# The even layer's output projection begun with the attention's half of its contraction, and the convolution's layer norm written behind that half

## The chip, the cores and the metric

The kernel runs on one core of a Trainium2 chip. The time is device microseconds (us) of that core for one execution. The engines are called PE (TensorE, the matmuls), PEld (its weight loads, which overlap the matmuls), DVE (VectorE), ACT (ScalarE), POOL (GpSimd) and SP (SyncE, which here only issues transfers).

## The reference: what is computed

Two residual layers on 512 positions of width 1024 and a final norm. The change lies in the first, the even layer. Its two halves are gated, concatenated and mapped back by one matrix:

```python
o_b = mla(...) * jax.nn.silu(z_b)
o_a = conformer_conv(glu_a, glu_g, conv_w, conv_b, ln_g, ln_b) * jax.nn.silu(z_a)
return x + (jnp.concatenate([o_b, o_a], axis=-1) @ w_out)

def conformer_conv(a, g, w, bias, ln_g, ln_b):
    u = a * jax.nn.sigmoid(g)
    u = dw_conv(u, w) + bias
    return jax.nn.silu(layer_norm(u, ln_g, ln_b))
```

`o_b` (the attention) and `o_a` (the convolution) are 512 x 1024 each, and `w_out` is 2048 x 1024: rows 0 to 1023 of it meet `o_b`, rows 1024 to 2047 meet `o_a`. All numbers are float32.

## The kernel before, in words

Each float32 operand of a projection is split into a rounded part and a rest (`hi`, `lo`), and a product is three matmuls: hi by hi, lo by hi, hi by lo. Weights come in slabs of 128 x 1024 (512 KB). `Weights._prepare` does for each slab: a transfer into `w_raw` on SP's queue (L84), a cast to `w_hi` on ACT (L87), and the rest `w_lo` on DVE or POOL (L88; in this projection by turns, odd and even places in the list of slabs). There are 2 buffers of `w_raw` and 3 each of `w_hi` and `w_lo`; `Weights.next` prepares one slab ahead of the one it hands out. So a slab's transfer waits until the `w_lo` of the slab two before is made, and its cast waits until PE has read the `w_hi` of the slab three before.

The output projection of the even layer is `mm_tm("oe", ...)`. It is done for the two halves h = 0, 1 of the 1024 output columns, with 8 slabs each; a slab holds two of the 16 blocks of 128 rows of the contraction. For each slab there are 4 tiles of 128 positions with 6 matmuls each (4 that read `w_hi`, 2 that read `w_lo`), 24 a slab. Slabs 0 to 3 of half h = 0 meet the attention's blocks (their split parts are the tiles `o_s`), slabs 4 to 7 the convolution's (`o_hi`, `o_lo`). Half h = 0 adds up in the banks `acc`, `acc`, `acc`, `cv`, half 1 in `sb`, `sb`, `tp`, `tp`.

Ahead of it stands the layer norm of the convolution's output, for 8 tiles of 128 channels (`ct`), L642 to L649: two DVE operations with one operand in PSUM (L644, L645), two on ACT (L646, L647), one on DVE with two operands in SBUF (L648), and the product with the gate on POOL (L649). Then each of the 8 tiles is split (`split_pages`: a cast on ACT at L358, a difference on DVE or POOL at L359). The gates themselves come from four matmul groups, the last of which (`gate_a(6)`, `gate_a(7)`) stand on PE right ahead of the projection.

The program is written in one order and each engine gets its instructions from a scheduler that may move them, but each engine then runs its list strictly in order, and waits where an instruction's inputs or buffers aren't ready. An instruction's wait holds up all behind it on that engine. SP's list is of the same kind.

Of the kernel before, what the change touches and what calls it, by code (L numbers as in the profile page):

```python
# [10 lines left out]
AF = mybir.ActivationFunctionType  # L11
ALU = mybir.AluOpType
# [91 lines left out]
OUT_E = (list(range(8)), [4, 5, 6, 7, 0, 1, 2, 3])  # L104
# [66 lines left out]
def trunk(ctx, tc, A, out, dbg=None):  # L171
    nc = tc.nc
    V, G, SC, T = nc.vector, nc.gpsimd, nc.scalar, nc.tensor
# [12 lines left out]
    def page(name, tag, dt=F32):  # L186
        return pg.tile([P, S], dt, name=name, tag=tag, bufs=npage[tag])
# [4 lines left out]
    def small(shape, name, bufs=2, dt=F32):  # L192
        return cp.tile(shape, dt, name=name, tag=name, bufs=bufs)
# [7 lines left out]
    def bank(tag):  # L201
        return ps.tile([P, S], F32, name=tag, tag=tag, bufs=banks[tag])

    def four(which):

        tags = [t for t in banks for _ in range(banks[t])]
        return tags[:4] if which == 0 else tags[4:]
# [61 lines left out]
    def along(cols, tag):  # L269

        b = bank(tag)
        for t in range(NT):
            T.matmul(b[:, t * P:(t + 1) * P], cols[:, t:t + 1].broadcast_to([P, P]), ident, start=t == 0, stop=t == NT - 1,
                     skip_group_check=True)
        return b

    def halves_square(part, x, h):

        j = small([P, S], "junk", bufs=1, dt=BF16)
        SC.activation(j, x[:, h * S:(h + 1) * S], AF.Square, accum_out=part[:, h:h + 1])  # L280
        if h == 0:
            mean_eps(part[:, 2:3], part[:, 0:1], D)
        else:
            V.tensor_scalar(part[:, 3:4], part[:, 1:2], 1.0 / D, part[:, 2:3], op0=ALU.mult, op1=ALU.add)
# [10 lines left out]
    def big(name):  # L295
        return bg.tile([P, KT, S], F32R, name=name, tag="big", bufs=2)

    def normT(x_tiles, gain, parts, tags):

        hi, lo = big("xT_hi"), big("xT_lo")  # L300
        for t in range(NT):
            r, tt = rstd(x_tiles[t], parts[t]), slice(t * P, (t + 1) * P)
            for h in range(2):
                c, hh, kk = page("xn", "keep"), slice(h * S, (h + 1) * S), slice(4 * h, 4 * h + 4)
                V.scalar_tensor_tensor(c, x_tiles[t][:, hh], r, gain[h], op0=ALU.mult, op1=ALU.mult)
                tp = transposed([c[:, k * P:(k + 1) * P] for k in range(4)], tags[t % 2][h])
                split_psum(hi[:, kk, tt], lo[:, kk, tt], tp.rearrange("p (k l) -> p k l", k=4))
        return [hi[:, k] for k in range(KT)], [lo[:, k] for k in range(KT)]
# [9 lines left out]
            T.matmul(a, l, r, start=n == 0, stop=n == 3 * kk - 1)  # L318
        return a

    def mm_tm(key, xT, nslabs, n, tags, last=1):


        xh, xl = xT
        accs = [bank(t) for t in tags] if nslabs > last else [None] * NT
        steps, k0 = [], 0
        for s in range(nslabs):
            w = W.next(key)
            steps.append((k0, *w))
            k0 += w[0].shape[1]  # L330
            if nslabs - last <= s < nslabs - 1:
                continue
            for t in range(NT):
                if accs[t] is None:
                    accs[t] = bank(tags[t])
                tt = slice(t * P, (t + 1) * P)
                for i, (k1, wh, wl) in enumerate(steps):
                    kk = range(wh.shape[1])
                    seq = [(x[k1 + k][:, tt], wh[:, k]) for k in kk for x in (xh, xl)]
                    seq += [(xh[k1 + k][:, tt], wl[:, k]) for k in kk]  # L340
                    end = s == nslabs - 1 and i == len(steps) - 1
                    for c, (l, r) in enumerate(seq):
                        T.matmul(accs[t][:, :n], l, r, start=k1 == 0 and c == 0, stop=end and c == len(seq) - 1)  # L343
                if s == nslabs - 1:
                    yield t, accs[t]
            steps = []
# [6 lines left out]
    def split_pages(src, new, pair=None):  # L353

        hs, ls = [], []
        for n, o in enumerate(src):
            hi, lo = (b[:, n] for b in pair) if pair and n < KT else (new(), new())
            SC.copy(hi, o)  # L358
            (V if n % 3 else G).tensor_tensor(lo, o, hi.bitcast(F32), op=ALU.subtract)  # L359
            hs.append(hi)  # L360
            ls.append(lo)
        return hs, ls
# [23 lines left out]
    for t in range(NT):  # L386
        for h in range(2):
            j = small([P, S], "junk", bufs=1, dt=BF16)
# [6 lines left out]
    for b in range(2):  # L395
        for t, a in mm_tm("qkv", xg, 3, 336, four(b)):
            SC.activation(qkv[t][:, b * 336:(b + 1) * 336], a[:, :336], AF.Copy, scale=r4[:, t:t + 1])

    rb = along(r4, "cv")
    xT = [], []  # L400
# [22 lines left out]
    for nm, o, w in (("q_norm", 0, 384), ("kv_norm", 384, 256)):  # L423
        ss = small([P, 4], "ss")
        rs = small([P, 4], "rs")
        for t in range(NT):
            j = small([P, S], "junk", bufs=1, dt=BF16)
# [20 lines left out]
    lg = cp.tile([P, 4, 8], F32, name="lg")  # L448
# [4 lines left out]
    def glu():  # L453

        pa, pgt = mm_cm("a", xT), mm_cm("g", xT)
        ut = page("u", "keep")
        SC.activation(ut, pgt, AF.Tanh, scale=0.5)
        V.scalar_tensor_tensor(ut, ut, 1.0, pa, op0=ALU.add, op1=ALU.mult)
        return ut
# [36 lines left out]
    def up_proj():  # L496

        q_tm = pg.tile([P, NT, 2, 192], F32, name="q_tm", tag="m6", bufs=2)
        v_tm = pg.tile([P, NT, 256], F32, name="v_tm", tag="v", bufs=2)
        for t, a in mm_tm("uq", cT["q_norm"], 2, 384, ("acc",) * 4, 2):  # L500
            SC.activation(q_tm[:, t].rearrange("p j d -> p (j d)"), a[:, :384], AF.Copy, scale=QS)
        for j in range(2):
            qr = q_tm[:, :, j, NOPE:2 * NOPE].rearrange("p t (i d) -> p t i d", i=2)
            rope(qr, qr, [P, NT, 2, ROPE], cosb, sinb, "q")
        for t, a in mm_tm("uv", cT["kv_norm"], 1, 256, ("acc",) * 4):
            SC.copy(v_tm[:, t], a[:, :256])
        return q_tm, v_tm
# [50 lines left out]
    def weigh(prs, allp, v_tm, h0):  # L558

        o = bank("acc")  # L560

        def mms(k):
            for j, pt in enumerate(allp[k]):
                T.matmul(o[j * HD:(j + 1) * HD], v_tm[:, k, (h0 + j) * HD:(h0 + j + 1) * HD], pt,  # L564
                         start=k == 0, stop=k == NT - 1, skip_group_check=True)

        for k in range(NT):
            if k + 2 < NT:
                allp.append(turn(prs, k + 2))
            mms(k)  # L570
        return o

    oT = [None] * 16
    u = [glu(), glu()]

    def gate_a(ct):
        z = mm_cm("za", xT)
        oT[8 + ct] = page("oT", "keep")
        gate(oT[8 + ct], z)
# [11 lines left out]
    for p in range(8):  # L591
# [22 lines left out]
        o = weigh(prs, allp, v_tm, h0)  # L614
# [8 lines left out]
    ob = split_pages(oT[:8], lambda: page("o_s", "att", F32R))  # L623
# [15 lines left out]
    lb = [along(rs[:, h], "sb") for h in range(2)]  # L639
    gate_a(6)  # L640
    gate_a(7)
    for ct in range(8):  # L642
        th, v, y = page("ln_th", "att"), page("ln_v", "att"), u[ct]
        V.tensor_tensor(y, y, lb[0], op=ALU.mult)  # L644
        V.tensor_tensor(y, y, lb[1], op=ALU.subtract)  # L645
        SC.activation(th, y, AF.Tanh, bias=lg[:, 1, ct:ct + 1], scale=lg[:, 0, ct:ct + 1])  # L646
        SC.activation(v, y, AF.Identity, bias=lg[:, 3, ct:ct + 1], scale=lg[:, 2, ct:ct + 1])  # L647
        V.scalar_tensor_tensor(v, th, 1.0, v, op0=ALU.add, op1=ALU.mult)  # L648
        G.tensor_tensor(oT[8 + ct], oT[8 + ct], v, op=ALU.mult)  # L649


    oh, ol = (a + b for a, b in zip(ob, split_pages(oT[8:], None, (big("o_hi"), big("o_lo")))))
    x1 = []
    for t in range(NT):
        x1.append(wide("x1"))
# [1 line left out]
    parts = [small([P, 4], "part", bufs=4) for _ in range(NT)]  # L657
    for h in range(2):
        c = slice(h * S, (h + 1) * S)
        o = [[p[2 * i + j] for i in OUT_E[h] for j in range(2)] for p in (oh, ol)]  # L660
        for t, a in mm_tm("oe", o, 8, 512, four(h), 2 if h else 1):
            V.tensor_tensor(x1[t][:, c], a, x1[t][:, c], op=ALU.add)
            halves_square(parts[t], x1[t], h)
    if dbg == "even":
# [13 lines left out]
    xT = normT(x1, gain, parts, (("cv", "acc"), ("acc", "acc")))  # L678
# [118 lines left out]
    for d in range(2):  # L797
        tp = transposed([d1[:, t, d * SH:(d + 1) * SH] for t in range(NT)], "tp", SH)
        cs = tmp("cs", "c5", 3)[:SH]
        for c in range(NT):  # L800
            o, i, z = cs[:, c * P:(c + 1) * P], tp[:, c * P:(c + 1) * P], ident[:SH]
            if d:
                o, i = o[:, ::-1], i[:, ::-1]
# [153 lines left out]
    last = []  # L957
# [20 lines left out]
    oh, ol = split_pages(oF[:13], more, (big("o_hi"), big("o_lo")))  # L978
    oh, ol = oh + [h for h, _ in last], ol + [l for _, l in last]
# [6 lines left out]
    for h in range(2):  # L986
        c = slice(h * S, (h + 1) * S)
        for t, a in mm_tm("oo", (oh, ol), 8, 512, four(h), 3 if h else 1):
            V.tensor_tensor(x1[t][:, c], a, x1[t][:, c], op=ALU.add)
            halves_square(parts[t], x1[t], h)  # L990
            if h:
                r = rstd(part=parts[t])
                for i in range(2):
                    o = slice(i * S, (i + 1) * S)
# [91 lines left out]
```

## Time and profile before

| | |
|---|---|
| median of 3 runs | 1000.29 us (997.64 to 1002.73) |
| the profiled execution, its own time | 1003.47 us |
| its span in the profile | 1001.7 us |
| mean granted TensorE clock | 0.978 of 2.4 GHz |
| PE busy | 93% of the span |
| DVE / ACT / POOL busy | 73% / 46% / 38% |

A row of a timeline below reads: start in us from the span's start, duration in us, engine, line, operation, out<-in, and how many instructions are merged in it; in brackets, where there is one, the idle time just ahead of it and what ended it. Engines are pipelined, so an instruction can start before the one ahead of it has ended.

### The profile page before, as it was taken

The numbers are of one execution on the slowest core, as the hardware profiler recorded it, in microseconds if no ns is written. First come the engines' busy times: TensorE is split into PE (matmuls) and PEld (weight loads), VectorE is DVE, ScalarE is ACT, GpSimd is POOL, SyncE is SP. The second block draws the span as 40 slices with busy tenths as digits, with TensorE's granted clock in tenths as the row PEclk, the third lists the DMA queues.
The fourth block names the chain that finished last, engine by engine and source line by source line (L and its number), as shares of the span: only waits on it lengthen the run. The fifth ranks groups of instructions, "written<-read, shape, count | busy, mean of one in ns | idle before, by whom it ended". The sixth has DMA issues, their size and how long they took to land. (4 is left out here: it accounts for less than half of the span.)

```text
span 1001.7 us, 12583 instructions
## 1 busy us (share of the span) xinstructions
PE 931.6 (93%) x4564; PEld 757.0 (76%) x4564; DVE 735.9 (73%) x1295; ACT 464.5 (46%) x916; POOL 384.0 (38%) x272
## 2 busy tenths in 40 slices
PE   7899999999999999699999999888869988999996
PEld 7887686686786777578889987676756876787885
DVE  4799989899898998922167537888998968956215
ACT  6646444454445453723143546456455555443312
POOL 0251743625428153531234354424433433445221
PEclk9999999999999999989999999989999998999999
DMA  8313322112213235033253533332333423322222
GB/s 302 101 29 111 55 68 70 49 40 84 69 25 115 74 31 170 22 127 105 81 173 92 168 125 96 95 110 83 92 120 84 122 90 102 109 101 82 92 84 84
DMA packets 42326, 95.99 MB, mean 96 GB/s; under 512 B 12136, under 2 KB 13800, under 8 KB 42264
## 3 DMA queue, kind: packets, MB, share of 16 engines
q1 hardware_dynamic: 42264, 95.19, 31.2%
q8 instruction: 36, 0.59, 0.2%
q14 instruction: 26, 0.21, 0.1%
HBM read 90.85 MB, written 4.33 MB: 95 GB/s over the span
## 5 line engine op out<-in xcount | busy, mean ns | idle before, releaser
L88 POOL TENSOR_TENSOR w_lo<-w_raw,w_hi 128x1024 fp32r<-128x1024 f32 (+2 forms) x68 | 159.5, 2347 | 267.2 <-ACT w_hi L87 181.2
L87 ACT CAST w_hi<-w_raw 128x1024 fp32r<-128x1024 f32 (+7 forms) x142 | 135.1, 952 | 221.8 <-PE acc L318 67.1
L318 PE MATMUL acc<-xT_hi,w_hi 128*128 128x512 f32 x544 | 222.0, 409 | 2.7 <-ACT xT_hi L404 2.7
L318 PE MATMUL acc<-xT_lo,w_hi 128*128 128x512 f32 x544 | 220.4, 406 | 0.4 <-POOL xT_lo L405 0.4
L88 DVE TENSOR_TENSOR w_lo<-w_raw,w_hi 128x1024 fp32r<-128x1024 f32 (+6 forms) x74 | 85.3, 1153 | 116.1 <-ACT w_hi L87 111.8
L318 PE MATMUL acc<-xT_hi,w_lo 128*128 128x512 f32 x544 | 142.7, 396 | 0.0
L479 DVE SCALAR_TENSOR_TENSOR cv<-u,pc,cv 128x497 f32<-128x497 f32 (+10 forms) x176 | 130.2, 740 | 10.0 <-ACT cv L468 7.7
L318 PEld LDWEIGHTS acc<-xT_hi,w_hi 128*128 128x128 f32 x544 | 105.3, 194 | 25.5 <-ACT xT_hi L404 2.9
L318 PEld LDWEIGHTS acc<-xT_lo,w_hi 128*128 128x128 f32 x544 | 105.3, 194 | 22.5 <-POOL xT_lo L405 0.8
L318 PEld LDWEIGHTS acc<-xT_hi,w_lo 128*128 128x128 f32 x544 | 101.9, 189 | 20.8
L477 POOL TENSOR_TENSOR side<-side 128x510 f32<-128x510 f32 (+3 forms) x56 | 77.9, 1391 | 4.7
L482 POOL TENSOR_TENSOR u<-cs,side 128x512 f32<-128x512 f32 x8 | 11.0, 1372 | 157.1 <-issue 149.9
L898 DVE SCALAR_TENSOR_TENSOR e<-e,nacs 128x128 f32<-128x128 f32 x96 | 50.8, 571 | 7.1 <-ACT e L897 7.1
L531 ACT ACTIVATE p<-sb,mx 128x512 f32<-128x512 f32 x64 | 43.4, 683 | 20.9 <-DVE mx L529 20.6
L476 POOL TENSOR_SCALAR side<-u,pc 128x510 f32<-128x510 f32 (+3 forms) x56 | 50.9, 910 | 4.7
L529 DVE TENSOR_REDUCE mx<-sb 128x1 f32<-128x512 f32 x64 | 41.7, 685 | 3.3 <-PE sb L527 2.6
L893 DVE SCALAR_TENSOR_TENSOR f<-cbm,dt,f 128x128 f32<-128x128 f32 x96 | 42.5, 488 | 0.4 <-ACT f L892 0.4
L897 ACT ACTIVATE e<-e,nacs 128x128 f32<-128x128 f32 x96 | 31.3, 391 | 21.6 <-DMA e<-acs 21.6
L266 PEld LDWEIGHTS tp<-kc,p 128*128 128x128 f32 x256 | 28.9, 140 | 16.0 <-ACT pt L554 10.7
L714 DVE SCALAR_TENSOR_TENSOR c<-acc,pc,c 128x510 f32<-128x510 f32 (+1 forms) x48 | 35.7, 744 | 6.7 <-ACT c L712 6.4
L527 PE MATMUL sb<-k_t,qk_hi 128*128 128x512 f32 (+1 forms) x128 | 39.5, 403 | 0.4 <-DVE k_t L257 0.3
L564 PE MATMUL acc<-pt,v_tm 128*64 128x512 f32 x128 | 37.6, 608 | 1.4 <-DVE pt L554 1.4
(336 smaller groups left out, 1927.4 us busy)
## 6 DMA issues: line engine op xcount, KB each, us to landing
w_raw<-in_w_cm_o SPq DMA_DIRECT2D x36, 512.0 KB, 3.5
w_raw<-in_w_cm_e SPq DMA_DIRECT2D x32, 512.0 KB, 3.5
e<-acs SPq DMA_DIRECT2D x24, 512.0 KB, 5.2
w_raw<-in_w_out_e SPq DMA_DIRECT2D x16, 512.0 KB, 3.5
w_raw<-in_w_out_o SPq DMA_DIRECT2D x16, 512.0 KB, 3.5
w_raw<-in_w_z SPq DMA_DIRECT2D x12, 384.0 KB, 3.2
xt<-in_xT SPq DMA_DIRECT2D x8, 256.0 KB, 5.4
x_t<-in_x SPq DMA_DIRECT2D x4, 512.0 KB, 6.5
```

What stands on the lines that cost most here:

```text
L87: nc.scalar.copy(hi, raw)
L88: eng.tensor_tensor(lo, raw, hi.bitcast(F32), op=ALU.subtract)
L318: T.matmul(a, l, r, start=n == 0, stop=n == 3 * kk - 1)
L476: G.tensor_scalar(t[:, o], ut[:, i], wt(j), 0.0, op0=ALU.mult, op1=ALU.add)
L477: G.tensor_tensor(side[:, o], side[:, o], t[:, o], op=ALU.add)
L479: V.scalar_tensor_tensor(c[:, o], ut[:, i], wt(j), c[:, o], op0=ALU.mult, op1=ALU.add)
L527: T.matmul(s, l[:, qs], r, start=n == 0, stop=n == 2)
L529: V.tensor_reduce(mx, s, axis=AX.X, op=ALU.max, negate=True)
L531: SC.activation(p, s, AF.Exp, bias=mx, accum_out=sums[:, q:q + 1])
L564: T.matmul(o[j * HD:(j + 1) * HD], v_tm[:, k, (h0 + j) * HD:(h0 + j + 1) * HD], pt, start=k == 0, stop=k == NT - 1, skip_group_check=True)
L893: V.scalar_tensor_tensor(f[:, cc], cbm[1][:, cc], dt[:, c, hb:hb + 1], f[:, cc], op0=ALU.mult, op1=ALU.add)
L898: V.scalar_tensor_tensor(e[:, cc], rb[:, 1, cc], nacs[:, c, hb:hb + 1], e[:, cc], op0=ALU.add, op1=ALU.min)
```

## The change

The layer norm and the split of the convolution's half become a function, and `mm_tm` calls it when it comes to slab 4 of half h = 0, just before it asks for that slab. So slabs 0 to 3 (and the preparation of slabs 1 to 4) stand ahead of the layer norm in the written program, and the four loads of the residual input (`x1`) do too. No instruction is added, removed or altered; the lists of ACT, DVE, POOL, PE and SP are rearranged.

```diff
-    def mm_tm(key, xT, nslabs, n, tags, last=1):
+    def mm_tm(key, xT, nslabs, n, tags, last=1, before=None):
...
         for s in range(nslabs):
+            if before and before[0] == s:
+                before[1]()
             w = W.next(key)
...
-    for ct in range(8):
-        th, v, y = page("ln_th", "att"), page("ln_v", "att"), u[ct]
...
-    oh, ol = (a + b for a, b in zip(ob, split_pages(oT[8:], None, (big("o_hi"), big("o_lo")))))
+    oh, ol = ob
+
+    def conformer():
+        for ct in range(8):
+            th, v, y = page("ln_th", "att"), page("ln_v", "att"), u[ct]
+            V.tensor_tensor(y, y, lb[0], op=ALU.mult)
+            V.tensor_tensor(y, y, lb[1], op=ALU.subtract)
+            SC.activation(th, y, AF.Tanh, bias=lg[:, 1, ct:ct + 1], scale=lg[:, 0, ct:ct + 1])
+            SC.activation(v, y, AF.Identity, bias=lg[:, 3, ct:ct + 1], scale=lg[:, 2, ct:ct + 1])
+            V.scalar_tensor_tensor(v, th, 1.0, v, op0=ALU.add, op1=ALU.mult)
+            G.tensor_tensor(oT[8 + ct], oT[8 + ct], v, op=ALU.mult)
+        for o, p in zip((oh, ol), split_pages(oT[8:], None, (big("o_hi"), big("o_lo")))):
+            o.extend(p)
...
-        o = [[p[2 * i + j] for i in OUT_E[h] for j in range(2)] for p in (oh, ol)]
-        for t, a in mm_tm("oe", o, 8, 512, four(h), 2 if h else 1):
+        o = [[p[2 * i + j] for i in OUT_E[1] for j in range(2)] for p in (oh, ol)] if h else (oh, ol)
+        for t, a in mm_tm("oe", o, 8, 512, four(h), 2 if h else 1, None if h else (4, conformer)):
```

What this makes of the engines' lists is shown at three places. In the lists of the changed kernel the layer norm's lines L644 to L649 are numbered L649 to L654, L343 is L345, and L358 and L359 are L360 and L361; L87 and L88 are the same in both.

DVE, from the first operation of the layer norm (`u<-u,sb`) on. Before:

```order
L644 TENSOR_TENSOR u<-u,sb 128x512 x2
L645 TENSOR_TENSOR u<-u,sb 128x512
L351 SCALAR_TENSOR_TENSOR oT<-oT,acc 128x512
L645 TENSOR_TENSOR u<-u,sb 128x512
L644 TENSOR_TENSOR u<-u,sb 128x512
L648 SCALAR_TENSOR_TENSOR ln_v<-ln_th,ln_v 128x512
```

And of the change:

```order
L649 TENSOR_TENSOR u<-u,sb 128x512 x2
L88 TENSOR_TENSOR w_lo<-w_raw,w_hi 128x1024
L353 SCALAR_TENSOR_TENSOR oT<-oT,acc 128x512
L650 TENSOR_TENSOR u<-u,sb 128x512 x2
L649 TENSOR_TENSOR u<-u,sb 128x512 x2
L653 SCALAR_TENSOR_TENSOR ln_v<-ln_th,ln_v 128x512
```

The `w_lo` of slab 1 now stands behind the second operation of the layer norm. Before, it is the 28th row counted from the place shown, ahead of the last difference of the split:

```order
L648 SCALAR_TENSOR_TENSOR ln_v<-ln_th,ln_v 128x512
L359 TENSOR_TENSOR o_lo<-oT,o_hi 128x512
L88 TENSOR_TENSOR w_lo<-w_raw,w_hi 128x1024
L359 TENSOR_TENSOR o_lo<-oT,o_hi 128x512
L88 TENSOR_TENSOR w_lo<-w_raw,w_hi 128x1024 x4
```

In the change the `w_lo` of slab 3 stands there among the layer norm's rows, between the seventh L649 and the fifth L653, and the `w_lo` of slab 5 behind all of the split.

POOL, from the first product with the gate (`oT<-oT,ln_v`) on. Before:

```order
L649 TENSOR_TENSOR oT<-oT,ln_v 128x512 x2
L359 TENSOR_TENSOR o_lo<-oT,o_hi 128x512
L649 TENSOR_TENSOR oT<-oT,ln_v 128x512 x3
L359 TENSOR_TENSOR o_lo<-oT,o_hi 128x512
L649 TENSOR_TENSOR oT<-oT,ln_v 128x512 x3
L359 TENSOR_TENSOR o_lo<-oT,o_hi 128x512
L88 TENSOR_TENSOR w_lo<-w_raw,w_hi 128x1024 x7
```

And of the change:

```order
L654 TENSOR_TENSOR oT<-oT,ln_v 128x512
L88 TENSOR_TENSOR w_lo<-w_raw,w_hi 128x1024
L654 TENSOR_TENSOR oT<-oT,ln_v 128x512 x2
L361 TENSOR_TENSOR o_lo<-oT,o_hi 128x512
L654 TENSOR_TENSOR oT<-oT,ln_v 128x512 x3
L88 TENSOR_TENSOR w_lo<-w_raw,w_hi 128x1024
L654 TENSOR_TENSOR oT<-oT,ln_v 128x512
L361 TENSOR_TENSOR o_lo<-oT,o_hi 128x512
L654 TENSOR_TENSOR oT<-oT,ln_v 128x512
L361 TENSOR_TENSOR o_lo<-oT,o_hi 128x512
L88 TENSOR_TENSOR w_lo<-w_raw,w_hi 128x1024 x5
```

The `w_lo` of slabs 2 and 4 have moved in among the eight products; before, that of slab 2 comes first behind them all.

PE, slab 1 of the projection. Before, and then of the change:

```order
L343 MATMUL acc<-w_hi,o_s 128x512 x12
L343 MATMUL cv<-w_hi,o_s 128x512 x4
L343 MATMUL acc<-w_lo,o_s 128x512 x6
L343 MATMUL cv<-w_lo,o_s 128x512 x2
L343 MATMUL acc<-w_hi,o_s 128x512 x4
```

```order
L345 MATMUL acc<-w_hi,o_s 128x512 x4
L345 MATMUL acc<-w_lo,o_s 128x512 x2
L345 MATMUL acc<-w_hi,o_s 128x512 x4
L345 MATMUL acc<-w_lo,o_s 128x512 x2
L345 MATMUL acc<-w_hi,o_s 128x512 x4
```

Before, all 16 matmuls of slab 1 that read `w_hi` stand ahead of the 8 that read `w_lo`; in the change the two kinds take turns, as in all the other slabs. The rest of PE's list is the same in both. On ACT the casts of slabs 2, 3 and 4 stand among the layer norm's rows instead of one (slab 2) there and the others behind the split. On SP the transfers of slabs 3 to 6 have moved ahead of two transfers of a gain vector (L677), with the rest of the list as before.

## Rows read from the trace of the kernel before

**Rows 1.** The page: busy time of each engine, share of the span and number of instructions.

```profile
PE 931.6 (93%) x4564; PEld 757.0 (76%) x4564; DVE 735.9 (73%) x1295; ACT 464.5 (46%) x916; POOL 384.0 (38%) x272
```

**Rows 2.** The waits of PE between 385 and 520 us: engine, tile and line that waited, who was waited for, total us, times, longest us.

```profile
PE acc L343 <- DVE w_lo L88: 9.6, 1, 9.6
PE cv L266 <- DVE xn L305: 0.4, 1, 0.4
```

**Rows 3.** The timeline of PE: the end of the last gate's matmuls (L318), slab 0 (from 407.95), slab 1 (from 413.39), slab 2 (from 430.33), slab 3 (from 436.74) and the start of half h = 1 (tile `sb`).

```profile
405.91 0.39 PE L318 MATMUL acc<-xT_lo,w_hi 128*128 128x512 f32 x1
...
407.95 1.07 PE L343 MATMUL acc<-w_hi,o_s 128*128 128x512 f32 x4
...
413.39 2.88 PE L343 MATMUL acc<-w_hi,o_s 128*128 128x512 f32 x12
416.11 1.07 PE L343 MATMUL cv<-w_hi,o_s 128*128 128x512 f32 x4
426.76 2.93 PE L343 MATMUL acc<-w_lo,o_s 128*128 128x512 f32 x6 [9.58 <-DVE w_lo L88]
429.48 1.05 PE L343 MATMUL cv<-w_lo,o_s 128*128 128x512 f32 x2
430.33 1.91 PE L343 MATMUL acc<-w_hi,o_s 128*128 128x512 f32 x4
...
436.74 1.07 PE L343 MATMUL acc<-w_hi,o_s 128*128 128x512 f32 x4
...
463.94 0.39 PE L343 MATMUL sb<-w_hi,o_hi 128*128 128x512 f32 x1
```

**Rows 4.** Stretches of the span: length, busy time of each engine with the number of instructions, granted clock, share of the DMA engines, GB/s.

```profile
417.00:431.00 14.00, 4.42 (x11) 3.38 (x11) 11.38 (x10) 5.49 (x9) 11.75 (x7) 0.68 0.17 59
431.00:442.00 11.00, 11.00 (x47) 8.99 (x47) 2.45 (x2) 2.42 (x4) 2.40 (x1) 0.94 0.53 176
442.00:464.00 22.00, 22.00 (x99) 18.23 (x98) 4.56 (x7) 6.03 (x9) 4.78 (x2) 1.00 0.33 104
464.00:486.00 22.00, 22.00 (x99) 18.22 (x98) 3.36 (x5) 5.57 (x9) 4.79 (x2) 1.00 0.30 96
```

**Rows 5.** The timeline of DVE: the layer norm from its first operation, its first and third L648, and the `w_lo` of slabs 1 (424.42) and 3 (431.28).

```profile
401.61 1.28 DVE L644 TENSOR_TENSOR u<-u,sb 128x512 f32<-128x512 f32 x2 [1.12 <-PE sb L273]
402.82 0.68 DVE L645 TENSOR_TENSOR u<-u,sb 128x512 f32<-128x512 f32 x1
...
405.21 0.68 DVE L648 SCALAR_TENSOR_TENSOR ln_v<-ln_th,ln_v 128x512 f32<-128x512 f32 x1
...
410.13 1.75 DVE L648 SCALAR_TENSOR_TENSOR ln_v<-ln_th,ln_v 128x512 f32<-128x512 f32 x1
...
424.42 2.28 DVE L88 TENSOR_TENSOR w_lo<-w_raw,w_hi 128x1024 fp32r<-128x1024 f32 x1
426.62 1.76 DVE L359 TENSOR_TENSOR o_lo<-oT,o_hi 128x512 fp32r<-128x512 f32 x1
431.28 1.23 DVE L88 TENSOR_TENSOR w_lo<-w_raw,w_hi 128x1024 fp32r<-128x1024 f32 x1 [2.90 <-ACT w_hi L87]
```

**Rows 6.** The timeline of POOL: the first product, the difference beside which DVE's third L648 stands, the next product, the last difference, and the `w_lo` of slabs 2 and 4.

```profile
405.97 1.30 POOL L649 TENSOR_TENSOR oT<-oT,ln_v 128x512 f32<-128x512 f32 x1 [12.28 <-DVE ln_v L648]
...
410.04 1.30 POOL L359 TENSOR_TENSOR o_lo<-oT,o_hi 128x512 fp32r<-128x512 f32 x1 [0.83 <-ACT o_hi L358]
411.97 1.30 POOL L649 TENSOR_TENSOR oT<-oT,ln_v 128x512 f32<-128x512 f32 x1 [0.63 <-DVE ln_v L648]
...
425.58 2.25 POOL L359 TENSOR_TENSOR o_lo<-oT,o_hi 128x512 fp32r<-128x512 f32 x1
427.80 2.81 POOL L88 TENSOR_TENSOR w_lo<-w_raw,w_hi 128x1024 fp32r<-128x1024 f32 x1
435.40 2.40 POOL L88 TENSOR_TENSOR w_lo<-w_raw,w_hi 128x1024 fp32r<-128x1024 f32 x1 [4.79 <-ACT w_hi L87]
```

**Rows 7.** The instructions of L648 and L649: count, shortest, median and longest ns, first and last start.

```profile
L648 DVE SCALAR_TENSOR_TENSOR ln_v<-ln_th,ln_v x8: 679/812/1754, 405.2 to 423.2; 128x512 f32<-128x512 f32 x8
L649 POOL TENSOR_TENSOR oT<-oT,ln_v x8: 1296/1306/1705, 406.0 to 424.0; 128x512 f32<-128x512 f32 x8
```

**Rows 8.** The timeline of ACT: the casts of slabs 1 (398.80), 2 (406.38) and 3 (430.20).

```profile
398.80 1.05 ACT L87 CAST w_hi<-w_raw 128x1024 fp32r<-128x1024 f32 x1 [6.99 <-PE acc L318]
...
406.38 1.06 ACT L87 CAST w_hi<-w_raw 128x1024 fp32r<-128x1024 f32 x1
...
430.20 1.04 ACT L87 CAST w_hi<-w_raw 128x1024 fp32r<-128x1024 f32 x1 [3.93 <-DMA w_raw<-in_w_out_e]
```

**Rows 9.** SP's queue: the issues around the projection's slabs (slab 2 at 393.72, slabs 3 to 9 from 426.73), its wait for the gain vector's page, and the time from issue to landing of L84's transfers between 380 and 480 us.

```profile
393.72 0.33 SPq L84 DMA_DIRECT2D w_raw<-in_w_out_e  x1
415.23 0.92 SPq L677 DMA_DIRECT2D gain<-in_norm_o  x2
426.73 23.34 SPq L84 DMA_DIRECT2D w_raw<-in_w_out_e  x7
...
SPq L677 <- POOL oT L649: 21.1, 1, 21.1
...
DMA to landing us min/median/max: 3.4/3.5/4.6
```

More of the change, by code (lines that the diff above doesn't have):

```diff
@@ L641, in trunk @@
     gate_a(7)
-    for ct in range(8):
-        th, v, y = page("ln_th", "att"), page("ln_v", "att"), u[ct]
[L644 to L649, printed above, removed]
-    oh, ol = (a + b for a, b in zip(ob, split_pages(oT[8:], None, (big("o_hi"), big("o_lo")))))
+    oh, ol = ob
[10 more added lines that the diff above has]
+            o.extend(p)
     x1 = []
```

## The prediction, written before the changed kernel ran

> **What bounds the kernel now.** I read the page first: PE is busy for 93% of the span [rows 1], so what is worth having is time in which PE waits or runs slow. Then the waits of PE around the change: between 385 and 520 us there are two, and only one is of any size, 9.6 us at L343 for a `w_lo` of L88 that DVE makes [rows 2]. Then PE's timeline [rows 3]. The reader is to see there that slab 0 takes 413.39 - 407.95 = 5.44 us, that PE does the 16 `w_hi` matmuls of slab 1, and then stands still from 417.2 to 426.76 us for slab 1's `w_lo`. The stretches tell the rest [rows 4]: from 417 to 431 us the granted clock is 0.68 (a mean over its two levels, 1.2 and 2.4 GHz), from 431 to 442 it is 0.94, and from 442 on it is 1.00 with PE busy in all of the 22.00 us. So after the idle time PE also runs at the lower level for some us.
>
> Why is that `w_lo` late? Its cast was done early, at 398.80 + 1.05 us [rows 8]. On DVE it stands behind the whole layer norm and all but one difference of the split, and begins at 424.42 [rows 5]. Nothing it needs is late; it is its place in DVE's list. The following slabs are late too: slab 2's `w_lo` is made on POOL from 427.80, behind the eight products [rows 6], and slab 3's transfer is issued at 426.73 [rows 9], when slab 1's `w_lo` frees its buffer.
>
> What all that costs: eight slabs at 5.44 us are 43.5 us, so half h = 0 could end at 407.95 + 43.52 = 451.47 us. Half 1 starts at 463.94 [rows 3]. The loss is 12.47 us. Of it 9.74 is idle (the last of slab 1's `w_hi` matmuls starts its four at 416.11, and 4 x 0.227 later, 0.227 being 5.44 / 24, PE is free at 417.02; to 426.76), 1.76 is that slab 1's eight `w_lo` matmuls took 430.33 - 426.76 = 3.57 instead of 8 x 0.227 = 1.81, and 0.97 is slab 2, 436.74 - 430.33 = 6.41 instead of 5.44: 12.47.
>
> **The change part by part.** It adds and removes no instruction, so it is worth what PE's waits become. PE's own list differs only within slab 1, where the same 24 matmuls stand in another order: nothing. What matters is when each slab's weights and, from slab 4 on, the convolution's split tiles are there, against a PE that comes to slab n at 407.95 + 5.44 n and to its first `w_lo` matmul four matmuls (0.91 us) later.
>
> Slab 1: `w_lo` stands behind DVE's first two L644, so from 402.82 [rows 5]; 1.23 us, made at about 404.1, needed at 414.3. It delays the layer norm. Ahead of the first L648 there now stand seven operations at 0.60 us (402.82 - 401.61 = 1.21 for two) and the `w_lo`, so it starts at 401.61 + 4.2 + 1.2 = 407.0 instead of 405.21, and POOL's first product, 0.76 later as before (405.97 against 405.21 [rows 5, 6]), at 407.75.
>
> Slab 2: its transfer was issued at 393.72 [rows 9] and is long there. Its cast needs the last gate's `w_hi` read, at 405.91 + 0.39 [rows 3], and took place at 406.38 before [rows 8]; some 0.5 us later now. `w_lo` is POOL's second instruction, 407.75 + 1.30 + 2.40 = 411.5 [rows 6]; needed at 419.7.
>
> Slab 3: transfer at 404.1, landed 3.5 us later [rows 9]; the cast needs slab 0's last `w_hi`, at about 413; `w_lo` on DVE at some 415 to 417; needed at 425.2.
>
> Now the layer norm and split, which feed slabs 4 to 7. The price of an operation here isn't its own duration alone. A free L648 takes 0.68 us (at 405.21), but the one at 410.13 takes 1.75 and ends at 411.88; POOL's difference beside it ends at 410.04 + 1.30 = 411.34, and POOL's next product begins at 411.97 [rows 5, 6]. So DVE's operations with two operands in SBUF and POOL's run one after the other, at 1.30 for POOL's and 0.54 for DVE's. Count so for before, from 405.97: eleven of POOL 14.3, seven L648 and five differences of DVE 12 x 0.55 = 6.6, one `w_lo` 1.23: 22.1, which gives 428.1 us. The last of them ended at 426.62 + 1.76 = 428.38 [rows 5]. The count holds.
>
> The Trainium skill says this as a rule, on the page "SBUF — State Buffer", section "Who interferes with whom": a VectorE instruction with two SBUF inputs and a GpSimd instruction that reads SBUF share a port pair, and whichever begins first keeps the other waiting for its whole length. The rows above agree. It is the rule that speaks against this change, since each `w_lo` put among the layer norm's rows then lengthens them by all of its time; without it POOL's own work would end at 426.9, by it the end is that of the count that follows.
>
> The same count after, from 407.75: 22.1 (slab 3's `w_lo` in place of slab 1's) and two of POOL's `w_lo`, 2 x 2.40 = 4.8 [rows 6]: 434.65 us for the last piece of the split. Slab 4's `w_lo` on POOL has behind it two products and two differences (5.2) and at least six of DVE's operations (3.3), so it is made at about 426.2; needed at 430.6, and its two tiles are split earlier still. Slab 5 is the tight one: its cast stands on ACT behind the last cast of the split, its `w_lo` on DVE behind the last difference, so it is made at 434.65 + 1.23 = 435.9; PE comes to it at 407.95 + 5 x 5.44 + 0.91 = 436.06. Slack 0.2 us. Slab 6's `w_lo` on POOL can be there 2.4 after the split's end and a cast (about 438.5), needed at 441.5. Slab 7's transfer waits for slab 5's `w_lo`: 435.9 + 3.5 + 1.05 + 1.23 = 441.7, needed at 446.9.
>
> So I take a wait of 0.3 us at slab 5. Its bounds: none, if POOL and DVE overlap at all; and, with a free operation's whole 0.68 for DVE's twelve, 12 x 0.13 = 1.6 more in the count (for before 429.7, later than it was), so 437.5 and a wait of 1.4. The far end: all of POOL's at the longest seen, 1.71 for a product [rows 7], 2.25 for a difference and 2.81 for a `w_lo` [rows 6], 8 x 0.41 + 3 x 0.95 + 2 x 0.41 = 6.9 more on top of the 0.3, though these long ones hold DVE's time already. I take 0.3 since the count at 1.30 met before's end within 0.3.
>
> Sum: 12.47 - 0.3 = 12.2 us less. Behind 451.7 half 1 and what follows shift as they are: from 442 to 486 PE had no wait and its weights came ahead of it [rows 2, 4]. The profiled execution took 1003.47 us, so 991.3 by it; it lay 3.2 above the median of the runs, 1000.29. For the median: **988.1 us**.
>
> **The rivals.**
> *The wait moves to slab 5 and is not small.* The count above can be short by the bounds given: a wait of 1.4 us gives 1000.29 - 11.1 = 989.2; the far 7.2, with the lower clock after it as before (1.76 + 0.97 = 2.7), a gain of 2.6 and 997.7. For it: the slack is 0.2 us. Against: the count's fit to before.
> *The gain is given back.* A transfer or list behind 464 us that doesn't shift would swallow it: 1000.3. For it: SP's list is in order and was held once before. Against: the weights of half 1 are paced by PE's own reads, with no wait of PE there [rows 2].
> *Slower, by SP's list.* The gain vector's transfer waited 21.1 us for a page that a product frees [rows 9]; now slab 7's transfer stands behind it. Slab 7 needs an issue by 446.94 - 5.8 = 441.1. Each us beyond costs one, and about 2.7 for the clock, so from an issue at 451 on the kernel is slower; if the page came free only behind half 0, at about 454, it would be 12.9 + 2.7 - 12.2 = 3.4 slower, 1003.7. For it: the old wait. Against: that wait ended at 415.23, and in the change all products are done by some 432.
>
> **How the numbers follow.** My forecast 0.80; the wait at slab 5 0.13; the gain given back 0.04; slower 0.03. Half a per cent, 5 us, is about what a measurement of this kernel can tell from no change, so faster is below 995.3: the forecast and most of the second case, 0.90; within half a per cent 0.07, slower 0.03. The forecast's own range is 988.1 with the spread of the runs before (-2.65, +2.44), 985.5 to 990.6. The range reaches up into the second case, to 994; what it leaves out above is the far part of that case (0.05) and the other two (0.07), and below 984 some 0.04.
>
> **What would show it right or wrong.** In the profile after: no wait of PE for a `w_lo` of L88 from 408 to 430 us; slabs 5.44 us apart, and half 1 starting near 451.7; the granted clock 1.00 from 408 to 452; the `w_lo` of slab 1 at 402.8 on DVE; the last difference of the split at about 434.6, some 6 us later than before; a wait of PE at slab 5, if anywhere. Wrong would be: a wait above 2 us at slabs 4 to 7, the end of the split behind 438, slab 7's transfer behind 441, or a new wait behind half 1.

## The result, and the profile after

The changed kernel takes **989.75 us** (median of 6 runs, 988.55 to 993.29) against 1001.5 us of the kernel before (6 runs, 997.64 to 1002.73): a ratio of 0.9893, 95% interval 0.9873 to 0.9913 (as recorded; here and below it is not exactly the quotient of the two medians), and 11.75 us less by the medians. The forecast was 988.1 in a range of 984 to 994, and 12.2 us less. The profiled execution took 989.05 us, its span is 987.2 (before 1003.47 and 1001.7).

The page of the kernel after, busy time of each engine; beside [rows 1] it shows that each engine has the same work, within 2.2 us:

```profile
PE 929.5 (94%) x4564; PEld 754.8 (76%) x4564; DVE 737.1 (75%) x1295; ACT 464.8 (47%) x916; POOL 385.2 (39%) x272
```

The waits of PE from 385 to 510 us, after:

```profile
PE cv L266 <- DVE xn L305: 0.4, 1, 0.4
```

The wait for a `w_lo` in [rows 2] is gone and none stands in its place. The timeline of PE after, the first matmuls of slabs 0 to 5 and of half h = 1:

```profile
407.11 1.07 PE L345 MATMUL acc<-w_hi,o_s 128*128 128x512 f32 x4
...
412.55 1.07 PE L345 MATMUL acc<-w_hi,o_s 128*128 128x512 f32 x4
...
417.99 1.07 PE L345 MATMUL acc<-w_hi,o_s 128*128 128x512 f32 x4
...
423.43 1.07 PE L345 MATMUL acc<-w_hi,o_s 128*128 128x512 f32 x4
...
428.87 0.39 PE L345 MATMUL acc<-w_hi,o_hi 128*128 128x512 f32 x1
...
434.31 0.39 PE L345 MATMUL acc<-w_hi,o_hi 128*128 128x512 f32 x1
...
450.63 0.39 PE L345 MATMUL sb<-w_hi,o_hi 128*128 128x512 f32 x1
```

Slab follows slab at 5.44 us. Half h = 0 lasts 450.63 - 407.11 = 43.52 us; in [rows 3] it lasts 463.94 - 407.95 = 55.99. So 12.47 us went there. The stretches after (columns as in [rows 4]) show PE busy throughout and the granted clock, the seventh entry, at 1.00, its upper level, where [rows 4] has 0.68 and 0.94:

```profile
417.00:431.00 14.00, 14.00 (x64) 11.58 (x63) 13.24 (x12) 6.66 (x11) 11.52 (x7) 1.00 0.33 113
431.00:442.00 11.00, 11.00 (x50) 9.11 (x49) 3.48 (x3) 4.62 (x5) 4.69 (x4) 1.00 0.36 116
```

The span is 14.5 us shorter, 2.0 more than that. 0.84 of it is that slab 0 started earlier, ahead of anything that the change touches; 1.2 lies behind half 1's start (1001.7 - 463.94 = 537.8 before, 987.2 - 450.63 = 536.6 after), in one execution of each. The difference of the medians, 11.75, is 0.72 less than the 12.47.

### The profile page after: what moved, and what is told of

It is laid out like the page before. It is cut to its first block, busy times and chain, and to the rows that moved or that the text cites. A ratio compares the mean times of both kernels' runs of the same rounds, so it can differ in the third digit from the quotient of the medians.

```text
span 987.2 us, 12582 instructions
## 1 busy us (share of the span) xinstructions
PE 929.5 (94%) x4564; PEld 754.8 (76%) x4564; DVE 737.1 (75%) x1295; ACT 464.8 (47%) x916; POOL 385.2 (39%) x272
## 5 line engine op out<-in xcount | busy, mean ns | idle before, releaser
L88 POOL TENSOR_TENSOR w_lo<-w_raw,w_hi 128x1024 fp32r<-128x1024 f32 (+2 forms) x68 | 160.4, 2361 | 254.2 <-ACT w_hi L87 155.1
L87 ACT CAST w_hi<-w_raw 128x1024 fp32r<-128x1024 f32 (+7 forms) x142 | 135.0, 952 | 202.9 <-PE acc L318 58.7
L318 PE MATMUL acc<-xT_hi,w_hi 128*128 128x512 f32 x544 | 223.1, 412 | 2.7 <-ACT xT_hi L406 2.7
L318 PE MATMUL acc<-xT_lo,w_hi 128*128 128x512 f32 x544 | 220.9, 407 | 0.0
L88 DVE TENSOR_TENSOR w_lo<-w_raw,w_hi 128x1024 fp32r<-128x1024 f32 (+6 forms) x74 | 83.8, 1132 | 96.8 <-ACT w_hi L87 92.5
L318 PE MATMUL acc<-xT_hi,w_lo 128*128 128x512 f32 x544 | 144.7, 400 | 0.0
L318 PEld LDWEIGHTS acc<-xT_hi,w_hi 128*128 128x128 f32 x544 | 106.0, 195 | 25.6 <-ACT xT_hi L406 2.9
L318 PEld LDWEIGHTS acc<-xT_lo,w_hi 128*128 128x128 f32 x544 | 105.6, 194 | 22.4 <-POOL xT_lo L407 0.4
L318 PEld LDWEIGHTS acc<-xT_hi,w_lo 128*128 128x128 f32 x544 | 103.3, 192 | 21.3
L904 DVE SCALAR_TENSOR_TENSOR e<-e,nacs 128x128 f32<-128x128 f32 x96 | 45.9, 520 | 9.6 <-ACT e L903 9.6
L899 DVE SCALAR_TENSOR_TENSOR f<-cbm,dt,f 128x128 f32<-128x128 f32 x96 | 47.4, 538 | 0.4 <-ACT f L898 0.4
L566 PE MATMUL acc<-pt,v_tm 128*64 128x512 f32 x128 | 37.6, 608 | 1.5 <-DVE pt L556 1.5
```

The costliest lines, as they stand in the source:

```text
L87: nc.scalar.copy(hi, raw)
L88: eng.tensor_tensor(lo, raw, hi.bitcast(F32), op=ALU.subtract)
L899: V.scalar_tensor_tensor(f[:, cc], cbm[1][:, cc], dt[:, c, hb:hb + 1], f[:, cc], op0=ALU.mult, op1=ALU.add)
L904: V.scalar_tensor_tensor(e[:, cc], rb[:, 1, cc], nacs[:, c, hb:hb + 1], e[:, cc], op0=ALU.add, op1=ALU.min)
```

## The experiments

**The theory** is the prediction's: a slab's `w_lo` waits for its place in the lists of ACT, DVE and POOL behind the layer norm and the split; if PE isn't to wait, every slab that PE reaches before the split ends must be prepared ahead of it or within it; and DVE's two-operand operations and POOL's run one after the other. **The rivals** tested: that the single wait for slab 1's `w_lo` is all the cost; that idle time alone, and not the lower clock after it, is lost; and that DVE and POOL overlap, so that the end of the split has far more room than the count says.

The runs were made on other chips, on which the kernel before takes 1007.72 us (the first four runs) or 1008.19 us (the last three) and slab 0 starts at 412.6 to 415.0 us, some 5 to 7 later than in [rows 3], because of the stages ahead. So each is compared with its own runs of before, and places in half h = 0 are counted from slab 0's first matmul. "Half 0" is the time from there to half 1's first matmul: 55.99 us before, 43.52 after. The kernel before has no profile on those chips; its 55.99 is that of [rows 3]. What half 0 gains against it agrees with what the medians gain within 1.2 us, but for e2_prep2 (5.40 and 3.58).

| run | median, us | ratio to before, 95% interval | half 0 | idle of PE in it | the rest of the loss |
|---|---|---|---|---|---|
| before (its profile) | 1001.5 | 1 | 55.99 | 9.58 | 2.89 |
| e1_prep1 | 1003.55 | 0.9960, 0.9933 to 0.9987 | 51.88 | 5.61 | 2.75 |
| e2_prep2 | 1004.14 | 0.9973, 0.9949 to 0.9997 | 50.59 | 5.27 | 1.80 |
| e3_three | 1000.74 | 0.9933, 0.9904 to 0.9962 | 49.70 | 1.21 + 1.63 | 3.34 |
| e4_heavy | 1003.40 | 0.9947, 0.9924 to 0.9970 | 51.71 | 4.09 + 1.14 | 2.96 |
| e5_change | 994.53 | 0.9858, 0.9819 to 0.9898 | 43.52 | none | none |
| e6_fill | 1008.07 | 0.9999, 0.9976 to 1.0023 | 56.60 | none | none, 13.06 of added matmuls |
| e7_dve_wlo | 995.67 | 0.9882, 0.9852 to 0.9912 | 43.52 | none | none |

The idle time is the figure in a row's brackets, and the last column is half 0 less 43.52 less the idle time. The prediction, which counts 0.227 us a matmul, has 9.74 and 2.73 for the same wait of before.

### One slab, or two, prepared early: e1_prep1 and e2_prep2

In the kernel before, with the layer norm left where it was:

```diff
     gate_a(6)
     gate_a(7)
+    W.fetch(2)
```

> The kernel before with one line more: slab 1 of the projection is prepared (transfer, cast, w_lo) ahead of the layer norm in the written program; the projection itself stays behind it. DVE's list then has slab 1's w_lo behind the second operation of the norm, and the scheduler has moved slab 2's cast and w_lo in among the norm's rows as well. Theory (a slab's wait is the place of its weights in the lists of ACT, DVE and POOL): PE's wait at slab 1 is gone and comes back at slab 3, whose cast on ACT now stands behind the split's last cast, at 429 to 431 us, where PE wants it at 424.3: a wait of 6 to 7.7 us and up to 2.7 for the lower clock. So only some 3 us of the 12.5 are won: 997 to 1000 us. Rival 1 (the one wait seen in the trace is the cost): without it 12 us less, 989 to 991. Rival 2 (the place of the projection in the written program matters, not its weights'): no change, 1001.5.

And the same with `W.fetch(3)`:

> As the run with slab 1 prepared early, but slabs 1 and 2 stand ahead of the norm in the written program. Theory: the wait is still slab 3's, as its cast is still behind the split, so no more than 0.5 us better than with slab 1 alone: 997 to 1000 us. Rival 1: 989 to 991. Rival (each slab prepared early wins its equal share of the 12.5 us): 4 x 12.5 / 4 parts, two of them 6 us, 995.

The timeline of PE in e1_prep1 at the only wait of half 0, the start of slab 3:

```profile
436.92 2.08 PE L343 MATMUL acc<-w_hi,o_s 128*128 128x512 f32 x4 [5.61 <-ACT w_hi L87]
```

ACT of e1_prep1 at that place, the last cast of the split and the casts of slabs 3 and 4 (the added line shifts the numbers of the layer norm by one, L650 is the product):

```profile
435.30 0.62 ACT L358 CAST o_hi<-oT 128x512 fp32r<-128x512 f32 x1 [1.05 <-POOL oT L650]
435.83 1.99 ACT L87 CAST w_hi<-w_raw 128x1024 fp32r<-128x1024 f32 x2
```

And PE in e2_prep2:

```profile
436.39 2.08 PE L343 MATMUL acc<-w_hi,o_s 128*128 128x512 f32 x4 [5.27 <-ACT w_hi L87]
```

The wait for slab 1 is gone in both and comes back two slabs on, now for a cast, which stands on ACT behind the last cast of the split. So the single wait isn't the cost: taking it away gives 4.11 us of half 0's 12.47 (e1_prep1) and 5.40 with one slab more (e2_prep2). The new wait, 5.61 us, is a little shorter than the 6 to 7.7 expected. The second slab shortened it by only 0.34, within the 0.5 expected; the rest between the two, 0.95, lies in the slower matmuls behind the wait, and why they cost less in e2_prep2 isn't shown. Their medians (4.2 and 3.6 us below before) can't be told from each other.

### The layer norm called one slab earlier: e3_three

```diff
-        for t, a in mm_tm("oe", o, 8, 512, four(h), 2 if h else 1, None if h else (4, conformer)):
+        for t, a in mm_tm("oe", o, 8, 512, four(h), 2 if h else 1, None if h else (3, conformer)):
```

> The changed kernel with the norm called one slab earlier, ahead of slab 3: slabs 0 to 3 are prepared ahead of it, slab 4 isn't. Theory: PE has no wait in slabs 1 to 3 and comes to slab 4 at 428.9 to 429.7; slab 4's cast stands behind the split's last cast on ACT and its w_lo behind the split's last difference on POOL, so it waits some 2 us for the cast and 2 more for the w_lo, and loses up to 2.7 to the clock if that falls: 4 to 7 us of the 12 are lost again, 993.5 to 997 us. Rival (what counts is that the attention's four slabs are covered; slab 4 waits for the norm in any case): as the change, 989 to 991.

The timeline of PE in e3_three in slab 4: its first tile up to the second wait, the matmuls behind that wait, and the fourth tile (from 444.61):

```profile
435.77 0.50 PE L345 MATMUL acc<-w_hi,o_hi 128*128 128x512 f32 x1 [1.21 <-ACT w_hi L87]
436.11 0.40 PE L345 MATMUL acc<-w_hi,o_lo 128*128 128x512 f32 x1
436.35 0.40 PE L345 MATMUL acc<-w_hi,o_hi 128*128 128x512 f32 x1
436.58 0.40 PE L345 MATMUL acc<-w_hi,o_lo 128*128 128x512 f32 x1
438.61 1.22 PE L345 MATMUL acc<-w_lo,o_hi 128*128 128x512 f32 x2 [1.63 <-POOL w_lo L88]
439.63 0.63 PE L345 MATMUL acc<-w_hi,o_hi 128*128 128x512 f32 x1
440.06 0.63 PE L345 MATMUL acc<-w_hi,o_lo 128*128 128x512 f32 x1
...
444.61 0.40 PE L345 MATMUL cv<-w_hi,o_hi 128*128 128x512 f32 x1
444.85 0.40 PE L345 MATMUL cv<-w_hi,o_lo 128*128 128x512 f32 x1
```

Slab 4 is now the one that comes behind the split, and PE waits for its cast and for its `w_lo`: 2.84 us. But half 0 loses 6.18, half of what the change won. The other 3.34 can be read off the starts: behind the second wait matmuls follow each other at 440.06 - 439.63 = 0.43 us, and at 444.85 - 444.61 = 0.24 where the clock is back. So the place of the call matters to the slab: at slab 4 nothing waits, at slab 3 half of the gain is gone.

### The serial count stretched: e4_heavy

In the change, a product on POOL behind each product with the gate, into a page that nothing reads any more; the output isn't touched:

```diff
             G.tensor_tensor(oT[8 + ct], oT[8 + ct], v, op=ALU.mult)
+            G.tensor_tensor(th, oT[8 + ct], v, op=ALU.mult)
```

> The changed kernel with eight products more on POOL: behind each product with the gate the same product is made again into a tile that nobody reads. The output is unchanged, and the lists of DVE, ACT and PE are the same as in the change. Serial count of the prediction (DVE's operations with two operands in SBUF and POOL's run one after the other): seven or eight products of 1.30 us more ahead of slab 5's w_lo, which was made at 434.3, so 443.4 to 444.7, where PE wants it at 435.2: a wait at slab 5 of 8 to 9.5 us and up to 2.7 for the clock, 998 to 1002 us. Rival (the engines overlap, each is busy for its own time): POOL's own nineteen of 1.30 and two of 2.40 from 406.9 on end at 436.4, slab 5's w_lo a little later, a wait of 1 to 3 us, 990.5 to 993.

The timeline of PE in e4_heavy, its two waits, at slab 4 and slab 5, and the matmuls behind the second:

```profile
441.77 1.22 PE L345 MATMUL acc<-w_lo,o_hi 128*128 128x512 f32 x2 [4.09 <-POOL w_lo L88]
...
451.00 0.73 PE L345 MATMUL acc<-w_lo,o_hi 128*128 128x512 f32 x2 [1.14 <-DVE w_lo L88]
451.57 0.40 PE L345 MATMUL acc<-w_hi,o_hi 128*128 128x512 f32 x1
451.80 0.40 PE L345 MATMUL acc<-w_hi,o_lo 128*128 128x512 f32 x1
```

POOL of e4_heavy, the first product with the gate, the sixth of the added products and slab 4's `w_lo`:

```profile
414.62 1.30 POOL L654 TENSOR_TENSOR oT<-oT,ln_v 128x512 f32<-128x512 f32 x1 [14.00 <-DVE ln_v L653]
...
437.38 1.59 POOL L655 TENSOR_TENSOR ln_th<-oT,ln_v 128x512 f32<-128x512 f32 x1
438.94 2.78 POOL L88 TENSOR_TENSOR w_lo<-w_raw,w_hi 128x1024 fp32r<-128x1024 f32 x1
```

DVE of e4_heavy, the `w_lo` of slab 5 behind the split:

```profile
448.63 2.31 DVE L88 TENSOR_TENSOR w_lo<-w_raw,w_hi 128x1024 fp32r<-128x1024 f32 x1
```

Slab 5's `w_lo` is made at 448.63 + 2.31 = 450.94, 36.1 us behind slab 0's start (414.86); in the change it is 434.33 - 407.11 = 27.2. Eight products at 1.30 moved it by 8.9 of their 10.4 us. The count had 36.3 to 37.6 us behind slab 0, the rival some 30.5 (436.4 + 1.2 - 407.11). Where the missing 1.5 went isn't shown; in the change POOL had idle pieces of 0.63 to 1.23 us ahead of five of its products, which added work can take first. The rows of POOL speak against the overlap by themselves: from its first product to the end of slab 4's `w_lo` it has no idle time above 0.1 us, and takes 441.72 - 414.62 = 27.1 us for thirteen operations of 1.30 and two of 2.40, which are 21.7.

The expectation missed the place and, with it, the time. It looked at slab 5 alone, but slab 4's `w_lo` on POOL has six of the added products ahead of it, came 26.9 us behind slab 0 instead of 18.0, and took most of the wait. PE wanted slab 5's `w_lo` 28.1 us behind slab 0 and got it 8.0 later; half 0 lasts 8.2 longer than in the change. So the slow matmuls behind the first wait cost next to nothing on top: they fell into time that PE would have spent waiting for slab 5's `w_lo`, where the expectation had added up to 2.7 for them. By the medians the kernel is 4.3 us below before, where the expectation had from 3.5 below to 0.5 above.

### The change again: e5_change

No edit.

> The change itself once more, beside the others. Theory: PE has no wait from slab 0 to the end of half 0, which takes 43.5 us from slab 0's first matmul (56.0 in the kernel before), so some 12.4 us less than before on the same chip, a ratio of 0.987 to 0.989. Rival (the first comparison was a matter of the chip): a ratio above 0.993, or half 0 longer than 45 us.

PE in e5_change, the first matmuls of slab 0 and of half 1:

```profile
414.97 1.07 PE L345 MATMUL acc<-w_hi,o_s 128*128 128x512 f32 x4
...
458.49 0.39 PE L345 MATMUL sb<-w_hi,o_hi 128*128 128x512 f32 x1
```

The same 43.52 us on another chip, and 13.7 us between the medians (0.9858, interval 0.9819 to 0.9898), which agrees with the first 0.9893. The expected ratio, 0.987 to 0.989, is a little above the measured one and inside its interval.

### The idle time filled with useless matmuls: e6_fill

In the kernel before; a bank that is written and not read:

```diff
             SC.copy(hi, o)
+            if pair and src[0] is oT[8] and n < 3:
+                f = bank("tp")
+                for _ in range(19):
+                    T.matmul(f, hi[:, :P], hi, start=True, stop=True)
```

> The kernel before, with 57 matmuls more whose result nobody reads, 19 on each of the first three split tiles of the convolution's half; on PE they stand within slab 1, behind its third w_hi matmul, and fill the time in which PE waited for slab 1's w_lo (57 x 0.227 = 12.9 us). All other lists are as before. Slab 1's other 21 matmuls stand behind them. Theory (about 2.7 us of the 12.5 are the lower clock, which follows PE's own idle time): the granted clock stays at 1.00 through the stretch and slabs 1 (its rest) and 2 run at 0.227 us a matmul; that takes off 2.7, and the 13 w_hi matmuls that now come behind the fill put 3 on, so half 0 takes 56 to 57 us and the kernel the same as before within 0.3%. Rival (slabs 1 and 2 are slow because their weights come late or the memory is contended): 0.45 us a matmul for the rest of slab 1, 4.7 us more, half 0 of 60 us or more, and the kernel 4 to 5 us slower than before.

PE in e6_fill, the 57 added matmuls, the next of slab 0, and slab 1's first that read `w_lo`:

```profile
416.56 13.22 PE L362 MATMUL tp<-o_hi 128*128 128x512 f32 x57
429.62 0.39 PE L343 MATMUL acc<-w_hi,o_s 128*128 128x512 f32 x1
...
433.93 0.62 PE L343 MATMUL acc<-w_lo,o_s 128*128 128x512 f32 x2
```

DVE in e6_fill, that `w_lo`:

```profile
431.06 2.31 DVE L88 TENSOR_TENSOR w_lo<-w_raw,w_hi 128x1024 fp32r<-128x1024 f32 x1
```

And one stretch of e6_fill:

```profile
431.00:442.00 11.00, 11.00 (x50) 9.13 (x49) 5.29 (x4) 2.69 (x3) 6.32 (x3) 1.00 0.42 124
```

The added matmuls stand nine matmuls into slab 0, earlier than the expectation had them, and slab 1's two kinds of matmuls take turns as in the change, but the run does what was wanted: slab 1's `w_lo` is made at 433.37 and first read at 433.93, with no wait, and the granted clock is 1.00 in the stretch where [rows 4] has 0.94. PE does 429.62 - 416.56 = 13.06 us more work in half 0 than before, and the kernel takes the same time (0.9999). So a wait of 9.74 us costs about what 13 us of work would, and the slow matmuls behind it go when PE's idle time goes. That they were slow because the memory was busy is spoken against by e7_dve_wlo below, where the same stretch has as much traffic as in [rows 4] (0.53 and 176 GB/s there), 50 matmuls and the upper clock:

```profile
431.00:442.00 11.00, 11.00 (x50) 9.09 (x50) 7.55 (x6) 4.06 (x5) 4.24 (x3) 1.00 0.52 175
```

### All of this projection's `w_lo` on DVE: e7_dve_wlo

In the change:

```diff
-        eng = nc.vector if key in EARLY or key in ("oe", "oo") and self.i % 2 else nc.gpsimd
+        eng = nc.vector if key in EARLY or key == "oe" or key == "oo" and self.i % 2 else nc.gpsimd
```

> The change with all w_lo of this projection made on DVE (1.22 us each when free) instead of by turns on DVE and POOL (2.40). Theory (DVE's operations with two operands in SBUF and POOL's run one after the other, and PE has no wait left): POOL's two w_lo among the norm's rows go, two of DVE's come, so the split ends some 2.5 us earlier counted from slab 0 (26.1 us behind it in the change, then about 23.6), and the time is that of the change within 0.3%. Rival (DVE is now the one that is full, with all the w_lo behind the norm on it): the split ends later than in the change, PE waits at slab 4 or 5, and the kernel is 2 to 6 us slower than the change.

POOL of e7_dve_wlo, the first product with the gate:

```profile
412.16 1.30 POOL L654 TENSOR_TENSOR oT<-oT,ln_v 128x512 f32<-128x512 f32 x1 [17.14 <-DVE ln_v L653]
```

DVE of e7_dve_wlo, the last differences of the split, and what follows them:

```profile
432.33 4.08 DVE L361 TENSOR_TENSOR o_lo<-oT,o_hi 128x512 fp32r<-128x512 f32 x3
436.34 2.35 DVE L88 TENSOR_TENSOR w_lo<-w_raw,w_hi 128x1024 fp32r<-128x1024 f32 x2
```

With slab 0 at 413.14, the split ends 432.33 + 4.08 - 413.14 = 23.3 us behind it, where the change has 26.1. A `w_lo` of 1.2 us on DVE in place of one of 2.4 on POOL, for two slabs, is 2.4 less in a count in which the two engines take turns; if they overlapped and POOL's list set the end, all of the 4.8 taken from POOL would be won. Measured: 2.8 from slab 0, but the first product stands 0.98 us ahead of slab 0 here and 0.25 in the change; counted from that product to its end the split takes 24.3 us and 26.3, so 2.1 of the 2.8 lie within it and 0.7 are an earlier start. That is near the first; that DVE's own list alone sets the end isn't excluded by this run, and what speaks for the shared count is POOL in e4_heavy. The time is that of the change (0.9882 and 0.9858, the intervals overlap): slab 5's room is larger, and that gains nothing, as PE has no wait there.

## Why the prediction held, step by step

**The loss of 12.47 us** (9.74 idle, 1.76 and 0.97 at the lower clock) was right: half 0 went from 55.99 to 43.52. e6_fill shows that idle time alone doesn't make it up. Of the 1.65 us between the forecast 988.1 and the measured 989.75, 1.21 is that the kernel before has a median of 1001.5 in six runs, and had 1000.29 in the three that the forecast started from.

**The `w_lo` of slab 1 and the late layer norm.** DVE after, `w_lo` of slab 1, the first L653, the last difference, and the `w_lo` of slab 5:

```profile
401.98 1.22 DVE L88 TENSOR_TENSOR w_lo<-w_raw,w_hi 128x1024 fp32r<-128x1024 f32 x1
...
406.10 0.68 DVE L653 SCALAR_TENSOR_TENSOR ln_v<-ln_th,ln_v 128x512 f32<-128x512 f32 x1
...
432.08 1.12 DVE L361 TENSOR_TENSOR o_lo<-oT,o_hi 128x512 fp32r<-128x512 f32 x1 [1.84 <-ACT o_hi L360]
433.12 1.21 DVE L88 TENSOR_TENSOR w_lo<-w_raw,w_hi 128x1024 fp32r<-128x1024 f32 x1
```

POOL after, the first product and the `w_lo` of slab 4:

```profile
406.86 1.30 POOL L654 TENSOR_TENSOR oT<-oT,ln_v 128x512 f32<-128x512 f32 x1 [13.99 <-DVE ln_v L653]
...
422.24 2.85 POOL L88 TENSOR_TENSOR w_lo<-w_raw,w_hi 128x1024 fp32r<-128x1024 f32 x1
```

All of these lie 0.84 us early, as slab 0 does. Less that, the steps said 401.98 for slab 1's `w_lo`, 406.16 for the first L653 and 406.91 for the first product: 401.98, 406.10 and 406.86 were measured.

**The serial count** said 434.65 - 0.84 = 433.81 for the end of the split; it ended at 432.08 + 1.12 = 433.20, against 428.38 in [rows 5], which lies 0.84 later by its slab 0: counted from there the layer norm and split end 5.7 us later, where the prediction had 6, and nobody waited for it. Slab 4's `w_lo` was made at 425.09 (said 425.4), needed at 428.87 + 0.91 = 429.78, with 4.7 us to spare. e4_heavy and e7_dve_wlo stretched and shortened the same count, to 36.1 us for slab 5's `w_lo` and 24.3 for the split. Both agree with the rule on the shared port pair that the prediction cites from the Trainium skill ("SBUF — State Buffer", "Who interferes with whom").

**The wait at slab 5** is the one term that was mis-sized: 0.3 us forecast, none there. Its `w_lo` was made at 433.12 + 1.21 = 434.33 and needed at 407.11 + 27.2 + 0.91 = 435.22; the room is 0.9 us where the prediction had 0.2, because its count was 0.6 too long. Its sum by itself gave no wait: the 0.3 is the miss of its count on before, and the slack would have taken 0.2 of it. So half 0 gained 12.47 where the sum said 12.2.

**SP's list**, the rival that would have made it slower. SP's queue after, slabs 3 to 6, the gain vector, and the slabs from 7 on:

```profile
403.22 22.23 SPq L84 DMA_DIRECT2D w_raw<-in_w_out_e  x4
425.50 0.90 SPq L683 DMA_DIRECT2D gain<-in_norm_o  x2
434.36 20.39 SPq L84 DMA_DIRECT2D w_raw<-in_w_out_e  x6
```

The gain vector's transfer went out at 425.50 behind slab 6's, and slab 7's at 434.36, when slab 5's `w_lo` freed its buffer, against a limit of 441.1 - 0.84 = 440.3. The rival that the gain is given back behind half 1 fell with the medians.

**The rival of a wait at slab 5** fell for this kernel. e4_heavy shows what a longer count does: with 9 us more in it slab 4's `w_lo` on POOL is late first, which the prediction had as safe (426.2 against 430.6), and slab 5's, 8.0 us late, sets the length of half 0.

**What stays open:** the 1.2 us by which the span behind half 1 was shorter in one profiled execution. PE's wait there for a tile `c` of the odd layer went from 11.6 to 9.0 us; whether that belongs to the change wasn't tried.

## What to carry to other kernels

Where a wait ends with an instruction whose inputs were ready long ago, look at what stands ahead of it on its engine, and ask for all the pieces that PE will reach before that block ends, not for the one that PE waits for: here preparing one or two of them early gave 33% and 43% of the gain in half 0, and preparing all that PE reached gave the whole. To see whether the block that was put off is late in turn, count DVE's operations with both operands in SBUF and POOL's as one queue, where the trace shows that they run one after the other. A wait of PE can cost more than its length: look at the spacing of the matmuls behind it, and at whether a later wait would have swallowed the slow ones.

## What the runs showed of the hardware that was not expected

What a wait costs beyond its own length does not follow that length: 2.89 us for an idle of 9.58, 2.75 for 5.61 but 1.80 for 5.27, and 3.34 for the two short ones of 1.21 and 1.63 in e3_three, more than the idle time itself; each is one profiled execution. In e3_three the four matmuls between the two idles are still 0.23 us apart at their end (436.35 to 436.58), those behind the second 0.43 (439.63 to 440.06). In e4_heavy the idle of 1.14 at slab 5 is followed by matmuls 0.23 apart (451.57 to 451.80). In the stretch from 442 us on, which has no idle time in it, e3_three still runs at a granted clock of 0.90, a mean over the two levels:

```profile
431.00:442.00 11.00, 8.16 (x28) 6.01 (x27) 8.14 (x5) 3.14 (x4) 6.93 (x4) 0.80 0.19 56
442.00:454.00 12.00, 12.00 (x49) 9.73 (x49) 1.22 (x1) 3.15 (x3) 4.06 (x2) 0.90 0.37 126
```
